# One decoder layer on one core: the keys' weights split during the values' products, first weight sums in another ring, a store and an activation moved, one head filled evenly

## The chip, the cores and the metric

The kernel runs on one core of a Trainium2 chip. The metric is device time in microseconds (us) of one execution, the median of several. TensorE (PE) multiplies matrices, ScalarE (ACT) and VectorE (DVE) work elementwise, GpSimd (POOL) does a few small jobs, and SyncE (SP) issues nearly all DMA transfers. Each engine runs its own instructions in the order in which the program lists them and waits on semaphores for the others.

## The reference

One decoder layer over 1024 tokens of width 1024, all in float32. Cut to what matters here:

```python
h = rms_norm(x, norm_mix_pre)
proj = h @ w_in          # 1024 x 7168: queries, keys, values, pool, memory queries, gate logits
q_d, k_d, v_d, u_p, q_m, gate_logits = split(proj)
# 8 heads; two softmax maps per head, distances as a bias, causal
s = einsum(q, k) * 64 ** -0.5 - slope[head] * (qpos - kpos);  s = where(qpos >= kpos, s, -big)
a = softmax(s)[map 0] - lam * softmax(s)[map 1];  a = rms_norm(a @ v_d) * (1 - lam_init)
gates = sigmoid(gate_logits)                       # 3 branches x 1024
mix = gates[0] * (a @ w_attn_branch) + gates[1] * pool_branch + gates[2] * memory_branch
x = x + rms_norm(mix @ w_out)
x = x + rms_norm((gelu(g) * v) @ w_down)           # [g | v] = conv3(rms_norm(x) @ w_up)
```

The change concerns the projections of values, queries and keys and the start of the attention. Nothing that is computed changes.

## The kernel before

**Float32 by halves.** A float32 operand is split by `split` into a high part, written by ACT as a copy in the matmul's format (L86, or L89 with a scale), and a low part, written by DVE as the rest (L87, L90). `mm3` (L94 to L96) then makes one product out of three matmuls: high by high, high by low, low by high. A *page* is the pair of high and low parts of one piece of weights. Pages live in the pool `wst`, in two rings named "wh" and "wl", two buffers each, used in turn by the counter `pages`; `wst` also has the ring "raw" (two buffers) for weights as loaded.

**Seven products.** Large projections use the seven-product scheme of Strassen and Winograd (`seven`, products named B11, T1, T2, B22, T3, B21, T4 in its order): `weight_sums` (L193 to L196, DVE) makes four sums of weight blocks, `product` splits a page and runs its twelve matmuls, and L211 to L223 bring the results from the accumulators into a tile.

**The stages around the change**, in order of time:
- *Gate pairs* (loop up to L622): sigmoid gates of the pool and memory branches, stored as `mixp_d` (L622).
- *Values* (L632 to L708, about 419 to 496 us). The value weights `vw` (four tiles of 1 MB) are loaded at L632. `value_product` runs seven products (B11, B21, T2, T1, T3, B22, T4), each with four pages (`vpage`) of twelve matmuls. Between them DVE makes sums of weights (`value_combination`, L657) and of results (L682 and others), and `value_out` splits results (`vhl`, `vout`) and stores them to `v_d` (L673).
- *Channels* (L710 to L744, about 496 to 623 us). `channels` loads two weight blocks (`rawq`, L715), makes their sums and runs `seven`: one pair for the keys of two heads, four pairs for the queries, one pair C_G for the first gate logits of the attention branch. The four sums lie in two tiles of ring "t" of pool `gq`, the ring that `value_out` uses for most of its `vhl` tiles too. `split_heads` splits a pair's result and stores it to `k_d` or `q_d` (L726). After each of the last three query pairs `key_weights` is called twice (heads 2 to 7): load a 512 KB block (`rawk`, L731), split it (`whl`, ring "g" of `gp_`), store 1 MB to `wk_d` (L734). These weights are read back during the attention, where the keys of heads 2 to 7 are computed. C_G's result `gq` is stored by POOL (L744).
- *Attention* (from about 623 us), head by head. POOL writes the table of distances `bias` (iota L756, then a mask L758); ACT scales it to `hbias` for each head (L763). `scores` runs the score matmuls into `pss` (L869, two maps), DVE adds `hbias` and finds the extreme (L872), ACT takes the exponential (L877). `combine` (L888 to L891) joins the maps, `turn_weights` transposes (L907), `weigh_values` multiplies by the values (L924), `head_norm` sums squares (L942). `weave` runs a head's stages and puts *fillers* between them: other work that keeps PE occupied. Head 0 has 22 stages and four fillers, two that load values and two that run the gate projection `gate(2)` (matmuls into `pg`); the parameter `over` = 10 has them all placed by the tenth stage. For the first scores SP loads `q`, `ks` (L798), then raw gate weights (L325), `v` and the next queries, in this order.

**What sets the order.** The code is written in loops; a scheduler places each instruction on its engine's list, and pools decide by their rings which tile waits for which. A tile of a ring can be written when all readers of the tile that had its buffer before are done, stores included. Completed transfers are counted on semaphores; SP's and ACT's transfers use eight of them in turn, DMAHW0 to DMAHW7, and the next transfer on one of them is issued only when the last one on it has landed. POOL's transfers have others.

## Time and profile before

| | |
|---|---|
| median of 3 runs | 1771.48 us (1771.41 to 1773.68) |
| the profiled execution | 1771.9 us, span 1770.0 us |
| PE busy | 1723.3 us, 97% of the span |
| DVE, ACT, POOL busy | 72%, 50%, 3% |
| mean granted TensorE clock | 0.993 of full speed |

The span runs from the first to the last instruction of the profiled execution; 1.9 us of its time lie around it. PE is busy nearly all the time, so a time is saved where PE waits or where its clock is low, and lost where either is new. The profile gives for each engine what it did, how long it sat idle ahead of a group of instructions and what it waited for (the *releaser*), and for each stretch the clock that was granted to PE.

### The profile page before, as it was taken

The page shows a single profiled execution, that of the slowest core. Times are in us where ns is not written, and L with a number is a line of the kernel's source. Part 1 is how long each engine was busy: PE and PEld are TensorE (multiplying, and loading weights), DVE is VectorE, ACT ScalarE, POOL GpSimd, SP SyncE. Part 2 cuts the span into 40 slices and gives each one's busy share as a digit, 9 for nine tenths or more (in the row PEclk, how much of TensorE's full clock was granted, in tenths as well). Part 3 has the DMA queues.
Part 4 walks back from the last instruction along what each step waited for, and adds up shares of the span by engine and source line. Part 5 has one row for each costly group of instructions (what it writes and reads, how often), then busy time and mean ns, then how long its engine had stood idle before and what let it go on. Part 6 is the DMA issues. An engine that isn't in the chain of part 4 may idle for free.

```text
span 1770.0 us, 22594 instructions
## 1 busy us (share of the span) xinstructions
PE 1723.3 (97%) x8138; PEld 1427.6 (81%) x8138; DVE 1274.0 (72%) x2221; ACT 885.7 (50%) x1544; POOL 45.9 (3%) x104
## 2 busy tenths in 40 slices
PE   6999999999989989999999999999999999999997
PEld 5888888888868768888887888888888888888886
DVE  7875875666556657888865557857888888878476
ACT  6434454434434457777743333555555555643452
POOL 0000000000000011111110000000000000000000
PEclk9999999999999989999999999999999999999999
DMA  7783544453357975765556482274333323483343
GB/s 243 250 321 129 181 149 131 163 162 120 109 161 254 288 207 165 195 162 156 158 169 226 156 251 72 102 227 153 93 122 119 110 88 107 172 305 101 112 141 138
DMA packets 230517, 294.94 MB, mean 167 GB/s; under 512 B 15761, under 2 KB 161414, under 8 KB 226950
## 3 DMA queue, kind: packets, MB, share of 16 engines
q1 hardware_dynamic: 226614, 285.08, 50.9%
q0 software_dynamic: 3792, 8.43, 1.3%
q8 instruction: 64, 1.05, 0.2%
q14 instruction: 47, 0.39, 0.1%
HBM read 201.62 MB, written 85.56 MB: 162 GB/s over the span
## 4 chain that ended last, share of the span: by engine, by line
PE 73%; issue 13%; DVE 4%; DMA 4%; ACT 2%; POOL 2%; SPq 0%; POOLq 0%; DVEq 0%; ACTq 0%
PE pa L94 8%; PE pa L96 8%; PE pa L95 8%; PE pb L94 5%; PE pb L96 5%; PE pb L95 5%; PE pya L96 2%; PE pe L96 2%; PE pe L95 2%; PE pe L94 2%; PE pya L94 2%; PE pya L95 2%; PE pd L94 2%; PE pd L95 2%; PE pd L96 2%
## 5 line engine op out<-in xcount | busy, mean ns | idle before, releaser
L86 ACT ACTIVATE wpage<-s 128x512 fp32r<-128x512 f32 x144 | 90.3, 628 | 105.9 <-DVE s L193 42.9
L87 DVE TENSOR_TENSOR wpage<-s,wpage 128x512 fp32r<-128x512 f32 x144 | 97.8, 689 | 45.1 <-ACT wpage L86 45.1
L1241 DVE SCALAR_TENSOR_TENSOR cvt<-gv,cols,cvt 128x1023 f32<-128x1023 f32 x88 | 112.5, 1278 | 15.7 <-ACT cvt L1237 15.7
L872 DVE CUSTOM_DVE_ANT_0 z<-pss,hbias 128x256 f32<-128x256 f32 (+7 forms) x128 | 94.8, 753 | 35.8 <-PE pss L869 27.1
L877 ACT ACTIVATE z<-z,mx 128x256 f32<-128x256 f32 (+7 forms) x128 | 99.1, 775 | 17.4 <-DVE mx L872 16.4
L94 PE MATMUL pa<-T,wpage 128*128 128x512 f32 x264 | 102.8, 389 | 0.8 <-DVE gv L244 0.8
L96 PE MATMUL pa<-T,wpage 128*128 128x512 f32 x264 | 102.7, 389 | 0.0
L95 PE MATMUL pa<-T,wpage 128*128 128x512 f32 x264 | 102.7, 389 | 0.0
L869 PE MATMUL pss<-ks,q 128*128 128x512 f32 (+5 forms) x384 | 89.7, 357 | 7.3 <-DVE mx L872 7.1
L86 ACT ACTIVATE page<-blk 128x1024 fp32r<-128x1024 f32 (+1 forms) x42 | 41.5, 990 | 85.9 <-PE pe L95 50.6
L869 PEld LDWEIGHTS pss<-ks,q 128*128 128x128 f32 x384 | 63.6, 193 | 18.4 <-DVE mx L872 14.0
L87 DVE TENSOR_TENSOR page<-blk,page 128x1024 fp32r<-128x1024 f32 (+1 forms) x42 | 47.7, 1136 | 39.3 <-ACT page L86 39.3
L86 ACT ACTIVATE wh<-raw 128x1024 fp32r<-128x1024 f32 (+1 forms) x46 | 41.9, 911 | 65.5 <-issue 16.6
L94 PE MATMUL pd<-page 128*128 128x512 f32 x176 | 68.6, 390 | 1.4 <-ACT row L1351 1.4
L96 PE MATMUL pd<-page 128*128 128x512 f32 x176 | 68.5, 389 | 0.0
L95 PE MATMUL pd<-page 128*128 128x512 f32 x176 | 68.5, 389 | 0.0
L94 PE MATMUL pa<-hT,wpage 128*128 128x512 f32 x168 | 65.7, 391 | 0.4 <-ACT gq L211 0.2
L96 PE MATMUL pa<-hT,wpage 128*128 128x512 f32 x168 | 65.4, 389 | 0.0
L95 PE MATMUL pa<-hT,wpage 128*128 128x512 f32 x168 | 65.4, 389 | 0.0
L924 PEld LDWEIGHTS poa<-aT,v 128*128 128x128 f32 x480 | 61.4, 192 | 4.2 <-ACT srow L944 2.0
L924 PE MATMUL poa<-aT,v 128*128 128x256 f32 (+1 forms) x480 | 63.6, 282 | 0.0
L87 DVE TENSOR_TENSOR wl<-raw,wh 128x1024 fp32r<-128x1024 f32 (+1 forms) x46 | 47.6, 1036 | 17.6 <-ACT wh L86 17.5
(409 smaller groups left out, 5048.3 us busy)
## 6 DMA issues: line engine op xcount, KB each, us to landing
q<-q_d SPq DMA_DIRECT2D x64, 256.0 KB, 4.8
wd<-in_w_down_dram SPq DMA_DIRECT2D x22, 512.0 KB, 5.3
tw_d<-wd SPq DMA_DIRECT2D x11, 1024.0 KB, 4.6
rawv<-in_w_up_dram SPq DMA_DIRECT2D x22, 512.0 KB, 5.6
rawu<-in_w_up_dram SPq DMA_DIRECT2D x22, 512.0 KB, 4.1
ff_d<-cvt SPq DMA_DIRECT2D x22, 512.0 KB, 4.4
blk<-ff_d SPq DMA_DIRECT2D x20, 512.0 KB, 7.1
br<-tw_d SPq DMA_DIRECT2D x20, 512.0 KB, 3.7
```

The lines of the kernel that those rows point to most:

```text
L86: nc.scalar.activation(out=hi, in_=src, func=AF.Copy)
L87: nc.vector.tensor_tensor(out=lo, in0=src, in1=hi.bitcast(F32), op=ALU.subtract)
L94: nc.tensor.matmul(o, ah, bh, start=first, stop=False, skip_group_check=onto)
L95: nc.tensor.matmul(o, ah, bl, start=False, stop=False, skip_group_check=onto)
L96: nc.tensor.matmul(o, al, bh, start=False, stop=last, skip_group_check=onto)
L869: nc.tensor.matmul(pss[:, i * H:i * H + m], q[:, j, c, ts], keys, start=(j == 0), stop=(j == 1))
L872: nc.vector.tensor_tensor_reduce(out=halves(z[:, 0:n]), in0=pss.rearrange("p (a m) -> p a m", a=2)[:, 0:parts, 0:m], in1=halves(biases[h][ ...
L877: nc.scalar.activation(out=z[:, 0:n], in_=z[:, 0:n], func=AF.Exp, scale=-1.0, bias=mx[:, c:c + 1], accum_out=sm if c else sums[:, h, t:t + 1])
L924: nc.tensor.matmul(po[:, qs], (vh, vl)[i][:, k, :], w[j][:, ws], start=(n == 0), stop=(n == len(terms) - 1))
L1241: nc.vector.scalar_tensor_tensor(out=cv[:, sh:], in0=u[:, 0:S - sh], scalar=w, in1=cv[:, sh:], op0=ALU.mult, op1=ALU.add)
```

## The change

1. `key_weights(h)` is called during the values instead of the channels: after B11 for head 2, then after B21, T2, T1, T3 and B22 for heads 3 to 7. The block is split in two halves into pages (`kpage`) of the rings "wh" and "wl", the rings of the value pages, and each half is stored on its own (512 KB, L666).
2. The four weight sums of the first pair (keys) lie in a tile `ss` of ring "y" of `gp_` instead of two tiles of ring "t".
3. The store of C_G's result to `gate_d` is issued from ACT's queue (L756 in the new numbering) instead of POOL's.
4. An activation `warm` (an exponential of one column) is written after the gate pairs.
5. `weave` loses `over`: head 0's four fillers are spread over its 22 stages.

```diff
-    def weave(stages, fillers, over=None):
+    def weave(stages, fillers):
-            want = min((i + 1) * len(fillers) // (over or len(stages)), len(fillers))
+            want = (i + 1) * len(fillers) // len(stages)
...
+        warm = small.tile([P, 1], F32, tag="sm", name="warm")
+        nc.scalar.activation(out=warm, in_=nlam, func=AF.Exp)
...
+        def key_weights(h):
+            raw = wst.tile([P, KT, P], F32, tag="raw", name="rawk", bufs=2)
+            nc.sync.dma_start(out=raw, in_=chunk(w_in, C_K + h * P))
+            for e in range(2):
+                page = wst.tile([P, 2, H4, P], F32R, tag=("wh", "wl")[pages[0] % 2], name="kpage")
+                pages[0] += 1
+                ks = slice(e * H4, (e + 1) * H4)
+                split(page[:, 0], page[:, 1], raw[:, ks])
+                nc.sync.dma_start(out=wk_d[h, :, :, ks], in_=page.bitcast(F32))
...
         value_product("B11", vblock(*A11), va, True)
+        key_weights(2)
...
         value_product("B21", vblock(*A12), vb, True)
+        key_weights(3)
...
         value_product("T2", vblock(*A11), va, False)
+        key_weights(4)
...
         value_product("T1", vblock(*A21), vb, True)
+        key_weights(5)
...
         value_product("T3", vblock(*A11), va, False)
+        key_weights(6)
...
         value_product("B22", vblock(*A12), vb, False)
+        key_weights(7)
...
-        def channels(c0, tag="g"):
+        def channels(c0, tag="g", ss=None):
...
-            s12, s43 = [gq.tile([P, 2, H4, P], F32, tag="t", name="s") for _ in range(2)]
-            seven(raws, (s12[:, 0], s12[:, 1], s43[:, 0], s43[:, 1]), hop, g)
+            if ss is None:
+                s12, s43 = [gq.tile([P, 2, H4, P], F32, tag="t", name="s") for _ in range(2)]
+                ss = (s12[:, 0], s12[:, 1], s43[:, 0], s43[:, 1])
+            seven(raws, ss, hop, g)
...
-        def key_weights(h):
-            raw = wst.tile([P, KT, P], F32, tag="raw", name="rawk", bufs=2)
-            nc.sync.dma_start(out=raw, in_=chunk(w_in, C_K + h * P))
-            whl = gp_.tile([P, 2, KT, P], F32R, tag="g", name="whl", bufs=3)
-            split(whl[:, 0], whl[:, 1], raw)
-            nc.sync.dma_start(out=wk_d[h], in_=whl.bitcast(F32))
-
-        split_heads(channels(C_K), k_d)
+        ss = gp_.tile([P, 4, H4, P], F32, tag="y", name="ss")
+        split_heads(channels(C_K, ss=[ss[:, j] for j in range(4)]), k_d)
         for h in range(0, NH, 2):
             split_heads(channels(h * P), q_d[h:h + 2], -0.125)
-            if h:
-                for e in range(2):
-                    key_weights(h + e)
...
-        nc.gpsimd.dma_start(out=gate_d[0:2].rearrange("e p s -> p e s"), in_=g)
+        nc.scalar.dma_start(out=gate_d[0:2].rearrange("e p s -> p e s"), in_=g)
...
-        weave(stages, fillers, 10 if h == 0 else None)
+        weave(stages, fillers)
```

The built programs show where this puts instructions. First, DVE at the step from the values' second product (B21) to the third (T2). Before, where `vw_3558` and `vw_3559` are T2's weights, `vpage_3705` to `vpage_3750` its four pages, and L682 adds B21's results:

```order
L87 TENSOR_TENSOR vpage_3682<-vw_3561,vpage_3682 128x512
L657 TENSOR_TENSOR vw_3559<-vw_3559 128x2x512
L87 TENSOR_TENSOR vpage_3705<-vw_3558,vpage_3705 128x512
L87 TENSOR_TENSOR vpage_3720<-vw_3558,vpage_3720 128x512
L682 TENSOR_TENSOR vtmp_3562<-ve_3569,vtmp_3562 128x512
L682 TENSOR_TENSOR vtmp_3562<-ve_3571,vtmp_3562 128x512
L682 TENSOR_TENSOR vtmp_3562<-ve_3570,vtmp_3562 128x512
L682 TENSOR_TENSOR vtmp_3562<-ve_3572,vtmp_3562 128x512
L87 TENSOR_TENSOR vpage_3735<-vw_3559,vpage_3735 128x512
```

Now T2's first pages are `vpage_3727` and `vpage_3742`, L698 is the same addition, and `kpage_3711` and `kpage_3715` are the halves of head 3's key weights:

```order
L87 TENSOR_TENSOR vpage_3694<-vw_3563,vpage_3694 128x512
L87 TENSOR_TENSOR kpage_3711<-rawk_3709,kpage_3711 128x512
L671 TENSOR_TENSOR vw_3561<-vw_3561 128x2x512
L87 TENSOR_TENSOR kpage_3715<-rawk_3709,kpage_3715 128x512
L698 TENSOR_TENSOR vtmp_3564<-ve_3571,vtmp_3564 128x512
L698 TENSOR_TENSOR vtmp_3564<-ve_3573,vtmp_3564 128x512
L698 TENSOR_TENSOR vtmp_3564<-ve_3572,vtmp_3564 128x512
L698 TENSOR_TENSOR vtmp_3564<-ve_3574,vtmp_3564 128x512
L87 TENSOR_TENSOR vpage_3727<-vw_3560,vpage_3727 128x512
L87 TENSOR_TENSOR vpage_3742<-vw_3560,vpage_3742 128x512
```

T2's first two low parts stood ahead of the four additions and stand behind them now.

Second, SP's list at the first scores, with what each transfer waits for. Before, `ks_4963` and `ks_4964` are head 0's keys for the two maps:

```order
L798 DMA ks_4963<-k_d 64x1024 [waits DMAHW2_49]
L798 DMA ks_4963<-k_d 64x1024 [waits DMAHW3_49]
L798 DMA ks_4964<-k_d 64x1024 [waits DMAHW4_49,DVE_49]
L798 DMA ks_4964<-k_d 64x1024 [waits DMAHW5_49]
L325 DMA raw<-in_w_in_dram 128x8x128 [waits DMAHW6_49]
L776 DMA v<-v_d 128x1024 [waits DMAHW7_49,PE_49]
```

Now they are `ks_4988` and `ks_4989`:

```order
L810 DMA ks_4988<-k_d 64x1024 [waits DMAHW1_49]
L810 DMA ks_4988<-k_d 64x1024 [waits DMAHW2_49]
L810 DMA ks_4989<-k_d 64x1024 [waits DMAHW3_49,DVE_49]
L810 DMA ks_4989<-k_d 64x1024 [waits DMAHW4_49]
L325 DMA raw<-in_w_in_dram 128x8x128 [waits DMAHW5_49]
L788 DMA v<-v_d 128x1024 [waits DMAHW6_49,PE_49]
```

And ACT's list at the same place, now (before, it is the same without the DMA, with the last L223, two `hbias`, the table load and the first exponential in a row):

```order
L215 ACTIVATE gq_4838<-pa_4845 128x512 [waits PE_49]
L86 ACTIVATE wpage_4944<-rawq_4836 128x512 [waits DMAHW1_49]
L223 ACTIVATE gq_4838<-pa_4845 128x512 [waits DVE_49,PE_49,Activation_49]
L756 DMA gate_d_91<-gq_4838 128x2x1024 [waits DVE_49,Activation_49]
L775 ACTIVATE hbias_4994<-bias_4973 128x1152 [waits Pool_49]
L775 ACTIVATE hbias_5042<-bias_4973 128x1152
L889 ACT_TABLE_LOAD
```

The store took a place among the transfers that count on DMAHW0 to DMAHW7: it counts on DMAHW4, and the second half of `ks_4989` now waits until that count shows the store landed. On POOL's list the DMA ahead of the iota is gone. The table load ahead of the first exponential is still there; `warm` has gone to ACT's 44th instruction, far ahead of the sigmoids' table load.

Third, PE in the middle of head 0. Before, `pg_5111` is the second half of the gate projection, `pss_5131` to `pss_5192` are scores:

```order
L95 MATMUL pg_5111<-hTl_111,wh 128x512
L96 MATMUL pg_5111<-hTh_109,wl 128x512
L869 MATMUL pss_5131<-ks_4963,q 128x320 x4
L869 MATMUL pss_5139<-ks_4964,q 128x320 x4
L94 MATMUL pg_5111<-hTh_109,wh 128x512
L95 MATMUL pg_5111<-hTl_111,wh 128x512
L96 MATMUL pg_5111<-hTh_109,wl 128x512
```

Nine more of these gate matmuls follow before the next transposes. Now the second half is `pg_5275`, and the scores are `pss_5142` to `pss_5230`:

```order
L881 MATMUL pss_5189<-ks_4989,q 128x384 x4
L95 MATMUL pg_5275<-hTl_111,wh 128x512
L96 MATMUL pg_5275<-hTh_109,wl 128x512
L94 MATMUL pg_5275<-hTh_109,wh 128x512
L881 MATMUL pss_5230<-ks_4988,q 128x448 x3
```

What stood in a block is now three matmuls at a time, up to the end of the head. The list of PE is the same in both programs again from early in head 1.

## Rows read from the trace of the kernel before

**Rows 1.** PE's waits, 420 to 670 us: total in us, times, longest

```profile
PE pss L869 <- DVE mx L872: 6.5, 3, 5.4
PE pb L94 <- ACT wpage L86: 6.4, 1, 6.4
PE pta L907 <- DVE aT L87: 1.2, 3, 0.7
PE pa L96 <- DVE wpage L87: 1.1, 1, 1.1
PE pa L94 <- ACT wpage L86: 1.1, 1, 1.1
PE pta L907 <- DVE z L891: 0.5, 1, 0.5
```

**Rows 2.** Stretches: us; PE, PEld, DVE, ACT, POOL busy; clock, DMA share, GB/s

```profile
460.00:480.00 20.00, 20.00 (x90) 16.57 (x89) 8.96 (x14) 8.65 (x15) 0.00 (x0) 1.00 0.20 54
...
500.00:505.00 5.00, 0.00 (x0) 0.00 (x0) 2.54 (x4) 1.23 (x2) 0.00 (x0) 0.80 0.85 236
505.00:510.00 5.00, 4.98 (x12) 3.89 (x13) 3.71 (x7) 1.86 (x3) 0.00 (x0) 0.52 0.01 3
...
560.00:610.00 50.00, 47.55 (x207) 38.13 (x206) 34.70 (x47) 27.43 (x40) 0.00 (x0) 1.00 0.97 323
...
628.40:636.40 8.00, 7.25 (x19) 5.41 (x20) 5.72 (x22) 6.84 (x17) 0.00 (x0) 0.52 1.03 351
...
660.00:664.00 4.00, 4.00 (x18) 3.62 (x19) 3.83 (x12) 3.86 (x10) 0.51 (x1) 0.57 0.99 227
```

**Rows 3.** Timeline, first pair: start, duration, instruction, [idle before <-releaser]

```profile
503.61 0.69 DVE L193 TENSOR_TENSOR s<-rawq 128x512 f32<-128x512 f32 x1 [1.29 <-DMA v_d<-vhl]
```

**Rows 4.** Key weights' splits: duration min/median/max in ns, first and last start

```profile
L86 ACT ACTIVATE whl<-rawk x6: 1054/1062/1073, 546.7 to 593.3; 128x1024 fp32r<-128x1024 f32 x6
L87 DVE TENSOR_TENSOR whl<-rawk,whl x6: 1215/1224/1227, 547.8 to 594.4; 128x1024 fp32r<-128x1024 f32 x6
```

**Rows 5.** Timeline of DVE at the end of the product B21

```profile
439.69 2.73 DVE L682 TENSOR_TENSOR vtmp<-ve,vtmp 128x512 f32<-128x512 f32 x4 [0.41 <-PE ve L96]
442.34 1.28 DVE L87 TENSOR_TENSOR vpage<-vw,vpage 128x512 fp32r<-128x512 f32 x2
```

**Rows 6.** Line 673's view: SP's 256 KB stores of values to v_d

```profile
DMA to landing us min/median/max: 2.3/2.6/3.7
```

**Rows 7.** Line 726's view: SP's 1 MB stores to k_d and q_d

```profile
DMA to landing us min/median/max: 3.9/5.3/6.2
```

**Rows 8.** Timeline of ACT late in the channels

```profile
603.81 0.63 ACT L86 ACTIVATE wpage<-rawq 128x512 fp32r<-128x512 f32 x1 [1.32 <-DMA rawq<-in_w_in_dram]
```

**Rows 9.** Timelines of ACT, POOL, DVE and PE at the attention's start

```profile
622.71 0.60 ACT L223 ACTIVATE gq<-pa 128x512 f32<-128x512 f32 x1 [8.90 <-PE pa L96]
626.89 2.22 ACT L763 ACTIVATE hbias<-bias 128x1152 f32<-128x1152 f32 x2 [3.58 <-POOL bias L758]
629.13 1.28 ACT L877 ACT_TABLE_LOAD   x1
...
623.62 0.88 POOL L744 DMA_DIRECT2D gate_d<-gq  x1 [572.63 <-ACT gq L223]
...
628.09 0.29 DVE L872 CUSTOM_DVE_ANT_0 z<-pss,hbias 128x128 f32<-128x128 f32 x1 [7.45 <-ACT hbias L763]
...
633.04 0.63 PE L94 MATMUL pg<-hTh,wh 128*128 128x512 f32 x1
```

**Rows 10.** Line 798's view: SP's loads of ks from k_d, 256 KB

```profile
DMA to landing us min/median/max: 4.3/10.7/11.6
```

**Rows 11.** DMA view, 420 to 670 us: the load of raw gate weights

```profile
raw<-in_w_in_dram SPq DMA_DIRECT2D x1, 512.0 KB, 5.9
```

**Rows 12.** Tile view of ks, all its loads of the run

```profile
DMA to landing us min/median/max: 2.2/4.0/11.6
```

**Rows 13.** Timeline of DVE in head 0

```profile
641.40 0.69 DVE L872 CUSTOM_DVE_ANT_0 z<-pss,hbias 128x512 f32<-128x512 f32 x1 [4.75 <-PE pss L869]
```

## The prediction

> **What bounds the kernel now.** I read the busy shares first: PE works in 97% of the span, so nothing that another engine saves counts unless PE waits for it. The second view is the list of PE's waits between 420 and 670 us, the stretch whose order the change touches [rows 1]; the list of PE is the same again after it. It holds three places. One wait of 6.4 us stands in the first pair of channels: the page of its first weight sum comes late. One of 5.4 us (of 6.5 in three) stands at the first scores, for DVE's extremes. Waits of 1.1 and 1.1 us stand late in the channels, and some 2.2 us of short ones (1.2, 0.5, and the remaining 0.5 beside the 5.4 and one of 0.6) lie at the end of head 0. The third view is the table of stretches [rows 2]: it shows what each wait costs beyond itself. Between 460 and 480 us, 90 matmuls take 20.00 us at full clock, 0.222 us each. After the first wait the granted clock is 0.52, near 1.2 GHz where 1.00 is 2.4 GHz, and 12 matmuls take 4.98 us. After the wait at the first scores it is 0.52 too, and in 660 to 664 us 0.57. All sums are made against the profiled execution, 1771.9 us; the median is 0.4 us lower, and I take that off at the end. 0.2%, or 3.5 us, is about what a measurement of this kernel can tell from no change.
>
> **The first pair's sums.** DVE's first sum starts at 503.61, released by the landing of a store of `vhl` [rows 3]: the sums lie in the ring that the last value stores still hold. In the new ring they wait for nothing of the last product; their raw weights are loaded later than before, but need to land only some 3 us ahead of the end of T4, and the order shows the sums ahead of T4's end. The wait goes whole: 6.4 us, and with it the clock's cost, 4.98 - 12 x 0.222 = 2.3 us [rows 1, 2]. **-8.7 us**. What is late next there is nothing on PE's path before the second product, whose page is split from sums that are ready. If the new ring's earlier readers should hold the sums, the value products before them hide up to 10 us of that.
>
> **The key weights' splits, moved.** Each costs ACT 1.06 and DVE 1.22 us [rows 4], six times; halved, they are twelve of about 0.64 and 0.69 (the value pages' own size). In the values DVE is busy 8.96 us of 20 and ACT 8.65 [rows 2], so the sum of 13.7 us of engine time (6 x 2.28) over 70 us hides behind PE, which stays dense. It costs only where a split stands in the order ahead of something PE is about to need:
> - *B21 to T2.* DVE's first addition of B21's results is released by PE's first finished accumulator at 439.69, and the four end at 442.42 [rows 5]; nine matmuls, 2.0 us, remain to PE at the first release, so PE reaches T2 near 441.4. Before, T2's first low parts were made by then. Now they stand behind the additions: the first is there at 442.42 + 0.64 = 443.06, and PE, with two high-by-high matmuls to spend (0.45 us), waits from 441.85, which is 1.2 us; the half key page ahead of the additions can add 0.7. I take 1.5; the ends are 0.5 (the scheduler's slack) and 2.9 (both key halves in the way).
> - *B11 to B21.* The second half of the value weights is loaded behind one more load, and the splits of head 2's halves stand ahead of the sum that follows: I take 0.5, ends 0 and 1.5. The other four steps have slack of a page; together 0.3.
>
> Together **+2.3 us**, ends 0.8 and 5.
>
> **Their stores, moved.** Six loads of 0.5 MB and twelve stores of 0.5 MB leave a stretch with a DMA share of 0.97 for one with 0.20 [rows 2]. SP gives each some 0.35 us, which nobody waits for as SP is not full there. But the pages lie in the rings of the value pages, so seven later pages each wait until a 512 KB store has landed. By the order such a page is wanted some 5.3 us after the store's issue (two pages of twelve matmuls, 12 x 0.222 = 2.7 us each). The trace does not show a 512 KB store there; the bounds are the 256 KB stores of the same stage, 2.3 to 3.7 us [rows 6], and the 1 MB stores of the next, 3.9 to 6.2 [rows 7]. I take 3.5, nearer to the former since the traffic is that of the former: no wait. At 6.2, five products would lose 0.9 each, 4.5 us; this is the high end.
>
> **Late in the channels.** ACT waits at 603.81 for a load of `rawq` [rows 8], which came late behind the key weights' loads and stores in the same ring and the same crowded stretch. With these gone the next pair's weights are loaded a pair ahead. 1.1 + 1.1 go [rows 1]; new is that C_G's first result waits until a `q_d` store has landed, 3.9 to 6.2 us against about 5.4 that it has: 0 to 0.8, taken as 0.2. **-2.0 us**.
>
> **The store on ACT, distances early.** Before, POOL's list was held until L223 was done, then by its own DMA: 0.88 us from 623.62, then iota and mask, and `hbias` ran at 626.89, and DVE began at 628.09 [rows 9]. Now iota and mask stand free, `hbias` follows L223 near 623.8, about 3 us earlier. That alone is worth 3.0 us. But the store now takes DMAHW4, and SP's second load of the second map's keys waits for it to land. Let T be the end of C_G's matmuls, near 622.6. L223 ends at T + 0.7; the store is issued by T + 1.0 and lands 3.9 to 6.2 later (5.0 taken) [rows 7]; the load is issued by T + 6.5 and lands 2.2 later at the least [rows 12], 4.3 at the least among the first loads [rows 10], 3.0 taken since the queue behind it is empty when it starts. So PE has the second map's keys at T + 9.5 (ends T + 7.6 and T + 12). From DVE's start to the gate matmuls it took 4.95 us before (628.09 to 633.04 [rows 9]), of which the first two extremes would now be done: 4.2 remain, so the gate matmuls start near T + 13.7. The raw gate weights, issued behind that load, agree: T + 7 + 5.9 [rows 11] + 1.0 for their split, T + 13.9. Before it was T + 10.4. In place of a gain of 3.0 the place loses **+3.1 us**, ends -3.0 (no wait) and +5.8. Queued behind the waiting load on SP are the raw gate weights, the values and the next queries; PE waits for the first two. The low clock after the wait is paid in either kernel.
>
> By the Trainium skill (DMA: Bandwidth & Descriptors, Anatomy of one DMA), a transfer on the POOL path takes about 2.0 us plus its bytes over 436 GB/s, an estimate of 4.4 us for 1 MB. Rows 7 have 5.3 as the median for stores issued by SP; with 4.4 in place of 5.0 this place would cost 2.5 and the time would be 0.6 lower.
>
> **Even filling.** Before, DVE sits idle 4.75 us for scores while PE runs gate matmuls in a block [rows 13], and at the end of the head PE waits for DVE, 2.2 us in all [rows 1], with the clock at 0.57 in four microseconds, at most 4.00 x 0.43 = 1.7 us of loss [rows 2]. Now the second half of the gate projection is spread, so DVE has its scores earlier and PE has matmuls left for the end. The first block still stands where it was, so the 4.75 us stay mostly; DVE remains 3.83 of 4.00 us busy there. Ends 0 and -3.9; I take **-2.7 us**.
>
> **The activation `warm`.** The table load of 1.28 us ahead of the first exponential [rows 9] is still in ACT's list, and `warm` stands hundreds of instructions ahead of the sigmoids, so it changes nothing: 0. The wait for `ks` would hide the load now anyway.
>
> **Sum.** -8.7 + 2.3 - 2.0 + 3.1 - 2.7 = -8.0. 1771.9 - 8.0 - 0.4 = 1763.5 us.
>
> **Rivals.**
> - *The store's wait is hidden.* If SP's load finds the store landed when PE wants the keys, the early `hbias` counts whole: -3.0 in place of +3.1, and the time is 1757.4. For it: SP's earlier loads might run late enough by themselves [rows 10]. Against: the order has the load directly behind loads that need only C_G's last low part. The Trainium skill (DMA: Bandwidth & Descriptors, Issuing engines are not separate DMA queues) says that issuing from several engines only saves the sequencer's issue time; by this the store's move alone would be worth the 0.88 us of POOL and no more, 1759.5. No row shows a DMA issued by ACT. Chance 0.2.
> - *The gains are eaten.* The even filling brings nothing, because DVE is as full in either order, and the steps between the value products cost 5 us: -8.7 + 5 - 2.0 + 3.1 = -2.6, 1768.9, and with the late ends at the first scores up to 1771.5. For it: DVE's 3.83 of 4.00 [rows 2]. Chance 0.17.
> - *The key pages hold the value products* (the other side). If a 512 KB store takes longer than 5.3 us to land while it shares the stage with loads and the stores of values, each of five products waits for the rest, and each wait can lower the clock. At 9 us this is 5 x 3.7 = 18.5 us: 1782. It decides from where 5 x (landing - 5.3) exceeds the 8.0 us: 6.9 us. Against: no SP store above takes over 6.2 us, even in the crowded stretch. Chance 0.07.
>
> **How the numbers follow.** The forecast has 0.56, with 1760 to 1767 as its own range; the first rival 0.20, the second 0.17, the third 0.07. Faster by over 0.2% (below 1768): the forecast, the first rival, and a little of the second: 0.78. Within 0.2%: most of the second, 0.15. Slower: the third, 0.07. The range from 1756.5 to 1771 takes in the first rival and nearly all of the second, and leaves out the third and the far ends.
>
> **What would show it.** Right: no wait of PE before the second product of the first pair, the clock at 1.00 there; `hbias` near 624; the second pair of score matmuls waiting for `ks` and not for DVE; the table load still ahead of the first exponential; no wait of a value page for a store. Wrong: value pages released by `wk_d` stores; a new wait at the first pair; PE waiting for DVE at the end of head 0 as long as before.

## The result, and the profile after

The changed kernel takes 1760.98 us (median of 4 runs, 1760.41 to 1761.98) against 1771.45 us of before on the same chip: a ratio of 0.9940, with an interval of 0.9923 to 0.9957. That is 10.5 us less; 1763.5 was forecast, with 1756.5 to 1771.0 as the range. The profiled execution took 1760.41 us with a span of 1758.4 us, 11.6 us under the span of before.

PE's waits from 415 to 665 us in the changed kernel (total, times, longest) answer to [rows 1]:

```profile
PE pss L881 <- DMA ks<-k_d: 8.7, 1, 8.7
PE vd L95 <- DVE vpage L87: 0.9, 1, 0.9
PE pss L881 <- DVE mx L884: 0.8, 2, 0.5
PE pa L94 <- ACT gq L211: 0.7, 1, 0.7
PE pta L919 <- DVE z L903: 0.7, 1, 0.7
PE pta L919 <- ACT sq L942: 0.2, 1, 0.2
```

The 6.4 us at the first pair are gone, as are the two of 1.1 late in the channels, and the short ones at head 0's end are fewer (the last four rows but the one for `gq`, 1.7 us, where 2.4 were). One wait is larger than before: the first scores now wait 8.7 us, and for a load of `ks`, not for DVE. The stretches (us; PE, PEld, DVE, ACT, POOL busy; clock, DMA share, GB/s) answer to [rows 2]:

```profile
440.00:460.00 20.00, 19.07 (x85) 15.44 (x84) 15.71 (x23) 10.56 (x20) 0.00 (x0) 1.00 0.86 268
460.00:480.00 20.00, 20.00 (x90) 16.57 (x89) 10.69 (x17) 10.98 (x19) 0.00 (x0) 1.00 0.56 175
...
500.00:505.00 5.00, 5.00 (x23) 4.13 (x22) 1.64 (x3) 2.60 (x5) 0.00 (x0) 1.00 0.78 219
505.00:510.00 5.00, 5.00 (x24) 4.13 (x23) 2.99 (x5) 2.47 (x5) 0.00 (x0) 1.00 0.95 258
...
618.00:622.00 4.00, 0.00 (x0) 0.00 (x0) 0.00 (x0) 0.54 (x3) 0.00 (x0) 0.56 0.69 150
622.00:626.00 4.00, 3.78 (x11) 2.83 (x12) 2.23 (x12) 2.58 (x8) 0.00 (x0) 0.50 1.01 326
```

PE runs through the first pair at full clock; 500 to 510 us hold 47 matmuls where before they held 12. The values' stretch moves more (a DMA share of 0.86 and 0.56 where 460 to 480 had 0.20), and PE stays dense there but for one wait. Only the first scores have a low clock, 0.50 when PE goes on.

To see where the time went I take the starts of PE's matmuls in both timelines as marks, since the order of PE's list hardly differs. Each line is the time from its mark to the next:

| from | before | after | difference | forecast |
|---|---|---|---|---|
| start to the values' first product | 418.9 | 419.1 | +0.2 | 0 |
| values, to the first product of the first pair | 76.9 | 78.7 | +1.8 | +2.3 |
| first pair, to its product B21 | 22.6 | 13.6 | -9.0 | -8.7 |
| to the product B21 of C_G | 98.7 | 96.4 | -2.3 | -2.0 |
| C_G's B21 to the first gate matmul | 16.0 | 18.9 | +2.8 | +3.1 |
| heads, to the branch projection | 311.6 | 308.0 | -3.5 | -2.7 |
| branch projection | 90.2 | 87.7 | -2.5 | 0 |
| the rest | 735.2 | 736.1 | +0.9 | 0 |

The five places that the prediction names are each within 0.9 us of their terms and sum to -10.2 where -8.0 was forecast. The branch projection, which the change does not touch, gave another 2.5; a second trace of before, below, settles whose they are.

The place that got worse, the first scores, as the timelines have it (start, us, instruction, idle before and releaser):

```profile
613.21 0.33 PE L881 MATMUL pss<-ks,q 128*128 128x128 f32 x2
622.22 4.60 PE L881 MATMUL pss<-ks,q 128*128 128x128 f32 x12 [8.67 <-DMA ks<-k_d]
626.62 0.63 PE L94 MATMUL pg<-hTh,wh 128*128 128x512 f32 x1
...
613.46 0.60 ACT L223 ACTIVATE gq<-pa 128x512 f32<-128x512 f32 x1 [9.81 <-PE pa L96]
614.09 0.39 ACTq L756 DMA_DIRECT2D gate_d<-gq  x1
614.53 2.22 ACT L775 ACTIVATE hbias<-bias 128x1152 f32<-128x1152 f32 x2 [0.47 <-ACT gq L223]
616.76 1.28 ACT L889 ACT_TABLE_LOAD   x1
618.05 0.40 ACT L889 ACTIVATE z<-z,mx 128x128 f32<-128x128 f32 x1
...
604.40 14.14 SPq L810 DMA_DIRECT2D ks<-k_d  x2
618.59 0.59 SPq L325 DMA_DIRECT2D raw<-in_w_in_dram  x1
```

`hbias` starts 1.1 us after L223 does, where [rows 9] has 4.2. But SP stands between its last two key loads until about 618, some 4 us after the store was issued on ACT at 614.09, the raw gate weights leave only at 618.59, and the keys let PE go on at 622.22.

### The profile page after: what moved, and what is told of

Same layout as the page of the kernel before. It is cut to its first block, busy times and chain, and to the rows that moved or that the text cites. A ratio compares the mean times of both kernels' runs of the same rounds, so it can differ in the third digit from the quotient of the medians.

```text
span 1758.4 us, 22637 instructions
## 1 busy us (share of the span) xinstructions
PE 1716.7 (98%) x8138; PEld 1424.0 (81%) x8138; DVE 1273.5 (72%) x2227; ACT 884.1 (50%) x1551; POOL 45.4 (3%) x103
## 4 chain that ended last, share of the span: by engine, by line
PE 82%; DVE 8%; DMA 4%; issue 3%; ACT 2%; SPq 0%; POOL 0%; DVEq 0%; ACTq 0%; POOLq 0%
PE pa L94 8%; PE pa L96 8%; PE pa L95 8%; PE pb L94 5%; PE pb L96 5%; PE pb L95 5%; PE pss L881 2%; PE pe L95 2%; PE pe L94 2%; PE pe L96 2%; PE pya L94 2%; PE pya L96 2%; PE poa L936 2%; PE pya L95 2%; PE pd L94 2%
## 5 line engine op out<-in xcount | busy, mean ns | idle before, releaser
L86 ACT ACTIVATE wpage<-s 128x512 fp32r<-128x512 f32 x140 | 87.7, 627 | 111.6 <-DVE s L193 37.4
L881 PE MATMUL pss<-ks,q 128*128 128x512 f32 (+5 forms) x384 | 90.7, 357 | 10.5 <-DMA ks<-k_d 8.7
L87 DVE TENSOR_TENSOR wl<-raw,wh 128x1024 fp32r<-128x1024 f32 (+1 forms) x46 | 47.6, 1035 | 19.0 <-ACT wh L86 18.9
```

What stands on the lines that cost most here:

```text
L86: nc.scalar.activation(out=hi, in_=src, func=AF.Copy)
L87: nc.vector.tensor_tensor(out=lo, in0=src, in1=hi.bitcast(F32), op=ALU.subtract)
L881: nc.tensor.matmul(pss[:, i * H:i * H + m], q[:, j, c, ts], keys, start=(j == 0), stop=(j == 1))
```

## The experiments

### The store on POOL again, in the changed kernel

```diff
-        nc.scalar.dma_start(out=gate_d[0:2].rearrange("e p s -> p e s"), in_=g)
+        nc.gpsimd.dma_start(out=gate_d[0:2].rearrange("e p s -> p e s"), in_=g)
```

> The changed kernel with C_G's store issued by POOL again; all else as changed. My theory: in the changed kernel the second load of the second map's keys waits on SP because it shares a completion count with the store on ACT, and PE's 8.7 us at the first scores are that. With the store on POOL the count is another, the wait for ks goes, POOL's iota stands behind the store again, and the place costs what it did before the change: a wait of about 5.4 us for the extremes, and the gate matmuls start 10.4 us after C_G's end in place of 13.2. Time about 2.8 us under the changed kernel's 1761.0, 1758.2 us. Rival (the keys are late because SP's queue is crowded, whoever issues the store): the wait for ks stays at 8 us or more and the time is 1761 or above.

1760.05 us (ratio to before 0.9941, 0.9929 to 0.9953). The wait for `ks` is gone, and the old one is back:

```profile
PE pss L881 <- DVE mx L884: 6.8, 4, 5.4
PE pa L94 <- ACT wpage L86: 1.0, 1, 1.0
```

From C_G's B21 to the first gate matmul it takes 16.0 us, 2.8 less than the changed kernel. So the wait was the store's place. In the whole time 0.9 us of it show, and the ratios cannot be told apart: 1.0 went to a page that came late in the channels here (the second row), and 0.5 to the heads. The clock accounts for the 0.5: over the 10 us from the first gate matmul its mean is 0.85 here and 0.90 in the changed kernel.

### The store on ACT, head 0's first queries loaded by POOL

```diff
-    queries(0, 0)
+    queries(0, 0, nc.gpsimd)      # the engine that issues the four loads
```

> The changed kernel with head 0's first four query loads issued by POOL in place of SP; the store stays on ACT. Nothing is taken from SP's crowd but four short loads, yet the counts turn by four, and the key loads share theirs with stores of queries that landed long ago. My theory (the shared count): PE's wait for ks goes, hbias stays early, the scores go on about 2.5 us after C_G's end, and the gate matmuls start 7 to 8 us after it in place of 13.2: about 1755.5 us. Rival (the keys are late because of the crowd on SP or in the DMA engines): at most 1 to 2 us less than the changed kernel, about 1760 us. A second rival is that POOL's loads land late: then PE waits for q, and the time is 1758 to 1763.

1759.56 us (0.9940, 0.9926 to 0.9953). The key loads are no longer held: they are all issued by 604.7, nearly nine us ahead of the store, and land in 4.3 to 6.8 us. The rows are PE's waits and the two landings:

```profile
614.46 0.41 PE L881 MATMUL pss<-ks,q 128*128 128x128 f32 x2 [1.89 <-issue]
618.91 1.20 PE L881 MATMUL pss<-ks,q 128*128 128x128 f32 x4 [4.04 <-issue]
...
DMA to landing us min/median/max: 4.3/6.4/6.8
...
DMA to landing us min/median/max: 3.8/5.4/12.2
```

The shared count is the cause, then: nothing was taken from SP's crowd but four short loads, and SP was no longer held between two key loads. But the second rival came true with it: POOL issued the queries at 604.5 to 607.1, into the raw weights and the values that SP was loading, and the last of them (the second landing row is that of all queries) took up to 12.2 us, so PE waited 1.9 and 4.0 us: two of these loads land at 614.4 and 618.7, where the waits end. The first gate matmul comes 5.9 us earlier than in the changed kernel, and the heads give back 3.5 of that. The clock accounts for 1.3 of the 3.5: its mean over the 10 us from the first gate matmul is 0.77, where the changed kernel has 0.90. The other 2.2 are not explained by any run.

### Only the store moved, in the kernel before

> The kernel before with only its store of C_G's result moved from POOL to ACT. In this program too the last of the four key loads shares its count with that store. My theory: slower by about 2.8 us than before, 1774.3 us, with PE waiting some 8 us for ks. Rival (the early distances outweigh it): 3.0 us faster, 1768.5 us.

1771.35 us against 1770.19 (1.0007, 0.9995 to 1.0019): no change that can be told, where 2.8 us were expected. PE's first wait at the scores is for `ks` here too:

```profile
PE pss L869 <- DMA ks<-k_d: 8.4, 1, 8.4
```

The first gate matmul comes 2.6 us later than in the trace of before, as expected, and the heads then take 2.3 us less than in that trace, and 1.4 less than in the second trace of before, below. The clock accounts for that. It is low behind the wait at the scores in each of these traces. Where the gate matmuls start later, more of that low clock has passed while PE waited. Here are the 10 us from the first gate matmul, before and then in this run:

```profile
633.04:643.04 10.00, 10.00 (x42) 7.85 (x42) 4.71 (x14) 4.04 (x12) 0.56 (x1) 0.85 0.45 155
...
635.01:645.01 10.00, 10.00 (x49) 8.00 (x48) 5.47 (x17) 4.20 (x11) 1.01 (x2) 1.00 1.06 234
```

Before loses 1.5 us to the clock in them (10.00 x 0.15; the second trace of before has 0.80, so 2.0), and this run nothing. In the first trace of before the clock also fell at the end of head 0 [rows 2], 1.7 us more; here it did not. By both traces the clock is worth more than what the heads gave back.

### The distances made early, loaded by SP; head 3's key weights later

```diff
+            bias0 = xa.tile([P, 1152], F32, name="bias0", bufs=1)     # in the memory stage
+            nc.gpsimd.iota(bias0, ...); nc.gpsimd.affine_select(out=bias0, ...)
+            nc.gpsimd.dma_start(out=bias_d, in_=bias0)
...
-        nc.scalar.dma_start(out=gate_d[0:2].rearrange("e p s -> p e s"), in_=g)
+        nc.gpsimd.dma_start(out=gate_d[0:2].rearrange("e p s -> p e s"), in_=g)
...
-    nc.gpsimd.iota(bias, ...); nc.gpsimd.affine_select(out=bias, ...)
+    nc.sync.dma_start(out=bias, in_=bias_d)
...
-        key_weights(3)                     # ahead of the additions of B21's results
+                if mid and k == 1:         # in value_product, for T2: after its second page
+                    key_weights(mid)
```

> The changed kernel with three edits: the table of distances is made by POOL during the memory stage, kept in device memory and loaded by SP; C_G's store is issued by POOL; head 3's key weights are split in the middle of T2 instead of ahead of it. My theory: no transfer at the first scores shares a count with the store, and nothing of the distances waits for it, so DVE has hbias 2.4 us after C_G's end and the keys of both maps, the gate matmuls start 6 to 7 us after C_G's end in place of 13.4, and the step from B21 to T2 is free again, 1.3 us: about 1755.5 us. Rival (head 0 is bound by DVE's and ACT's own chain of scores, so an earlier start is given back by its end): 1758.5 us.

1755.50 us (0.9912, 0.9898 to 0.9925), 5.5 us under the changed kernel and what the theory said to the tenth; the exactness is luck. At the first scores (PE, ACT, SP):

```profile
614.98 4.50 PE L886 MATMUL pss<-ks,q 128*128 128x128 f32 x12 [2.02 <-DMA ks<-k_d]
...
613.06 2.21 ACT L780 ACTIVATE hbias<-bias 128x1152 f32<-128x1152 f32 x2
...
601.63 0.32 SPq L776 DMA_DIRECT2D bias<-bias_d  x1
```

PE waits 2.0 us there in place of 8.7, and the first gate matmul comes 7.0 us after C_G's end where the changed kernel has 13.4. The heads take 308.6 us, nearly the changed kernel's 308.0, so the gain is kept this time. The values take 0.7 us less. Of the two theories it was the first. Three edits were made at once, so the whole time does not price them one by one; the marks do, as far as their places are apart.

### The same with `warm` behind the sigmoids

```diff
-        nc.scalar.activation(out=warm, in_=nlam, func=AF.Exp)
+        nc.scalar.activation(out=warm, in_=mix[:, 0, 0:1], func=AF.Exp)
```

> The kernel with the distances' table loaded (e7_table_loaded), in which the activation warm reads the last gate pair's result and so stands behind the sigmoids: the table of the exponential is loaded in the values, and no table load stands ahead of the first exponential. My theory: there, nothing hides the 1.28 us of the load any more, the first exponential and the gate matmuls behind ACT's split come 1.3 us earlier, and 0.5 to 1.3 us remain at the end of head 0: 1754.5 us against 1755.5. Rival (the wait of the second map's keys hides it there too): 1755.5.

1753.75 us (0.9912, 0.9898 to 0.9925): the ratio is that of the last, so the times do not tell the two apart. The trace shows what the load costs:

```profile
613.69 2.21 ACT L780 ACTIVATE hbias<-bias 128x1152 f32<-128x1152 f32 x2
615.80 0.39 ACT L894 ACTIVATE z<-z,mx 128x128 f32<-128x128 f32 x1
```

The first exponential follows `hbias` directly, 2.85 us after C_G's end where the last kernel has 4.26 (616.58 against 612.32). The first gate matmul does not come earlier (7.2 us after C_G's end against 7.0), since PE waits 2.1 us for the keys in this one too; from C_G's end to the branch projection it is 1.0 us less.

### The changed kernel without `warm`

> The changed kernel without the activation warm. My theory: no change, 1761.0 us, with the table load in the same place. Rival (the early load of the table spares something somewhere): about 1.3 us slower.

1761.59 us (0.9950, 0.9936 to 0.9963), no change that can be told, and the table load stands where it stood:

```profile
614.85 2.21 ACT L773 ACTIVATE hbias<-bias 128x1152 f32<-128x1152 f32 x2 [0.47 <-ACT gq L223]
617.09 1.28 ACT L887 ACT_TABLE_LOAD   x1
618.38 0.40 ACT L887 ACTIVATE z<-z,mx 128x128 f32<-128x128 f32 x1
```

### Only the sums' ring, in the kernel before

> The kernel before with the first pair's weight sums in the other ring and nothing else. My theory: the wait of 6.4 us and the low clock behind it are the ring alone, so all of the 8.9 us that the first pair gained in the changed kernel's trace comes: about 1761.5 us against 1770.2 of before on the last chip. Rival (the key weights' move is needed too, since the sums' raw weights share a ring with them): a wait of 3 us or more stays, 1765 us or above. A second rival is that the earlier end of the channels is given back at the first scores or at head 0's end: 1764 us.

1763.63 us against 1771.51 (0.9964, 0.9951 to 0.9978): 7.9 us by the medians, 6.4 by the ratio (3.9 to 8.7), so more than half of the whole change by either, from the place of one tile. It is less than the 8.9 us of the theory and near the second rival's 1764, though not by its way. The first pair takes 13.6 us to its B21, as in the changed kernel, so the ring alone took the wait and its clock away. 2.5 us are given back late in the channels, where the short waits of before are still there and the clock fell behind them in this execution, at a loss of 1.7 us (4.00 x 0.10 + 4.00 x 0.32):

```profile
596.00:600.00 4.00, 2.61 (x9) 1.82 (x10) 3.87 (x7) 2.50 (x5) 0.00 (x0) 0.90 1.02 376
600.00:604.00 4.00, 4.00 (x14) 3.20 (x13) 0.69 (x1) 1.12 (x2) 0.00 (x0) 0.68 1.02 247
```

### Only the key weights moved, in the kernel before

> The kernel before with the key weights' splits moved into the values and stored by halves, and nothing else. My theory: the values take 1.9 us more (the step from B21 to T2 and the later second half of the value weights), the late channels 2.4 us less, and the first pair's wait stays: 0.5 us faster than before, 1769.7 us. Rival (the first pair's wait comes from the crowd of transfers that the key weights' move thins out): 1763 us. Rival on the other side (value pages wait for the stores): slower than before by over 2 us.

1771.89 us against 1771.51 (1.0009, 1.0000 to 1.0018): by itself the move is worth nothing, or costs up to 3 us, where a gain of 0.5 was expected. Late in the channels it gains 2.5 us; the values take 2.3 more; and the first pair's wait grows. As before, its first sum waits for a store of `vhl`, which lands later now: the sum starts 9.4 us after the pair's first matmul (507.40 against 498.01), where it was 7.9:

```profile
PE pb L94 <- ACT wpage L86: 7.9, 1, 7.9
...
507.40 0.69 DVE L193 TENSOR_TENSOR s<-rawq 128x512 f32<-128x512 f32 x1 [1.97 <-DMA v_d<-vhl]
```

### Each half page stored twice

```diff
                 nc.sync.dma_start(out=wk_d[h, :, :, ks], in_=page.bitcast(F32))
+                nc.sync.dma_start(out=wk2_d[h, :, :, ks], in_=page.bitcast(F32))
```

> The changed kernel in which each half page of key weights is stored twice, the second time to memory that nobody reads, so that a page comes free only when both have landed. It prices the late landing. By the prediction's step (a page is wanted 5.3 us after its store is issued), landings of 9 to 10 us would cost five products 4 us each: some 1780 us. My theory now, from the changed kernel's landings of 6.3 us median and 9.1 at most without a wait of PE: ACT makes pages some 3 us ahead of PE's need, so PE waits only for what passes 9 us: 1761 to 1766 us.

1776.37 us against 1771.51 (1.0026, 1.0016 to 1.0036): 15 us over the changed kernel and slower than before, far above the 1761 to 1766 that I had come to expect and near the 1780 of the prediction's step, but not by its way. PE's waits in values and first pair:

```profile
PE pb L94 <- ACT wpage L86: 7.8, 1, 7.8
PE vd L95 <- DVE vpage L87: 2.0, 1, 2.0
PE vd L94 <- ACT vpage L86: 1.7, 1, 1.7
```

The values cost 5.0 us (83.7 against 78.7), most of it 2.8 more of waits, and 1.7 of a low clock behind the first of them (4.00 x 0.43, from 445 to 449 us). Three pages were held until a store had landed, a key page (8.9 us after its store was issued) and two value pages (4.9 and 5.7 us after the second store of each), and PE waited for none of these three directly; what made its two waits longer stays open. Landings of 9 us at a value page did not come about, so this run does not price them. The larger part, 10.0 us, is the first pair, whose wait is back though its sums lie in the new ring:

```profile
502.56 3.55 SPq L689 DMA_DIRECT2D v_d<-vhl  x4
506.16 0.87 SPq L737 DMA_DIRECT2D rawq<-in_w_in_dram  x1
...
511.72 0.69 DVE L193 TENSOR_TENSOR ss<-rawq 128x512 f32<-128x512 f32 x1 [1.02 <-DMA rawq<-in_w_in_dram]
```

The pair's second load of `rawq` leaves at 506.16, behind value stores on SP's list, and the first sum waits for it until 511.72. In the changed kernel the same load left at 487.31, and the first sum stood at 492.64. The other side is real, then, but it decides at SP's queue more than at the pages' ring.

### Only the even filling, in the kernel before; and the change without it

> The kernel before with head 0's fillers spread evenly and nothing else. My theory: the end of head 0 gains by itself, since the 2.2 us of waits for DVE and the low clock after them go: 3.5 us faster, 1768.0 us, ends 2.7 and 3.9. Rival (the gain at head 0 seen in the changed kernel comes from the later start of the scores, by which the transfers of head 0 and 1 have landed): within 1 us of 1771.5.

1769.54 us against 1770.19 (0.9990, 0.9980 to 1.0000), less than the theory, and at the edge of what can be told: between nothing and 3.5 us. The heads take 309.6 us to the branch projection, 2.0 less than in the first trace of before and 1.1 less than in the second, below. The theory that the low clock at the end of head 0 goes with the even filling is wrong: here it fell there all the same, as in the first trace of before and not as in the second.

```profile
662.00:666.00 4.00, 3.88 (x15) 3.23 (x16) 3.48 (x11) 2.18 (x7) 0.00 (x0) 0.57 0.62 250
```

That is 1.7 us (4.00 x 0.43). With it left out on both sides, the heads are 2.0 us shorter than in the first trace and 2.8 shorter than in the second.

> The changed kernel with head 0's four fillers placed by the tenth stage again; all else as changed. It prices the even filling inside the change. By the prediction it is worth 2.7 us: 1763.7 against 1761.0 of the changed kernel. By the traces of the kernels without it so far (65.4 to 66.0 us from the first gate matmul to the 48th key matmul of head 2 where the clock fell once, 67.1 in the trace of before where it fell a second time at the end of head 0, 63 with even filling) it is worth 1 to 2 us: 1762 to 1763. Rival (nothing, since the head's end waits for DVE in either): 1761.

1763.89 us (0.9963, 0.9951 to 0.9976) against 1760.98: 2.9 us by the medians, where the prediction had 2.7. The two ratios to before make it 4.1, and the run without `warm`, measured on the same chip, 2.3 (1763.89 - 1761.59). The heads take 310.6 us, 2.6 more than with even filling. So inside the change the filling is worth about what was forecast. In the kernel before, the whole time allows 0 to 3.5 us, so no other worth is shown there.

### The kernel before, a second time

> The kernel before once more, for a second trace. In the first one 384 matmuls of the branch projection came 0.2334 us apart after a wait of 0.5 us, where the traces of the changed kernel and of all the experiments have 0.2289, and the clock fell a second time at the end of head 0. If both belong to the kernel, they are there again; if they belong to that execution, the branch projection shows 0.2289, or head 0's end full clock, and the profiled execution is up to 3 us shorter.

1771.58 us, span 1769.7: 0.3 us under the first profiled execution, not 3. Yet both oddities of the first trace were that execution's: the branch projection runs at the usual spacing, and the clock did not fall at head 0's end. It fell late in the channels instead, behind the short waits there, and cost 3.4 us (8.00 x 0.43, the first row):

```profile
605.00:613.00 8.00, 6.86 (x18) 5.09 (x17) 3.93 (x7) 3.08 (x6) 0.00 (x0) 0.57 1.04 291
660.00:664.00 4.00, 2.76 (x17) 2.03 (x17) 3.93 (x7) 2.85 (x6) 0.00 (x0) 1.00 0.65 158
985.00:1000.00 15.00, 15.00 (x67) 12.33 (x66) 6.67 (x9) 4.44 (x7) 0.00 (x0) 1.00 0.51 155
```

With this trace as before, the stretches differ from the changed kernel's by 1.7 (values), -9.5 (first pair), -5.4 (late channels, with the low clock), +2.8 (first scores), -2.7 (heads) and -0.1 us (branch projection).

## Why the prediction was right, point by point

**The first pair.** -8.7 forecast, -9.0 and -9.5 measured against the two traces of before. The cause was the ring alone, as put (only the ring: the wait gone). What the prediction did not see is its condition: the raw weights must leave SP's queue in time, and with the stores doubled they did not.

**The splits in the values.** +2.3 forecast, +1.8 measured. The wait stands where it was put, at T2's first low part, 0.9 us where 1.5 was taken. The prediction's own row gives 0.9 without the half key page: nine matmuls, 2.0 us, from 439.69 are 441.7, and the text went on with 441.4. With head 3's key weights split in the middle of T2 this wait is gone, and the values take 0.7 us less than in the changed kernel, still 1.1 more than before.

**The stores' landing.** 3.5 us was taken for a store of 512 KB, and it held where a value page waited for one. Below are the view of all twelve stores, ACT's rows with the waits, and SP's rows with the stores (each row the two halves of one head, the second some 2.7 us behind the first):

```profile
DMA to landing us min/median/max: 3.6/6.3/9.1
...
461.67 0.63 ACT L86 ACTIVATE vpage<-vw 128x512 fp32r<-128x512 f32 x1 [1.16 <-DMA wk_d<-kpage]
472.82 1.29 ACT L86 ACTIVATE vpage<-vw 128x512 fp32r<-128x512 f32 x2 [1.43 <-DMA wk_d<-kpage]
...
458.54 3.24 SPq L666 DMA_DIRECT2D wk_d<-kpage  x2
469.42 3.23 SPq L666 DMA_DIRECT2D wk_d<-kpage  x2
```

ACT's four waits for these stores, 4.7 us in all, end 3.1 to 3.7 us after the stores were issued (461.67 - 458.54 and 472.82 - 469.42 for the first halves). PE takes up these two pages only at 465.11 and 475.99, and so never waited. The view's first line must not be read as a median of twelve: the trace has the landing of two of them, 9.1 and 3.6 us. The expectation for the doubled stores was built on that median. The two halves of head 2 took 9.1 and 9.2, since the move fills that stretch (a DMA share of 0.96 from 430 to 440 us, where before it was 0.39); they held two key pages for 1.1 us together, and no value page. So one sign of being wrong did show, value pages released by `wk_d` stores, but at ACT and not at PE. The other step, that a page is wanted 5.3 us after its store, was short: PE takes those pages up 6.6 us after the issue (465.11 - 458.54), and ACT needs 0.6 of that. The rival on the other side, 18.5 us for landings of 9 us, is not priced by any run; what it left out is SP's queue, where the doubled stores cost the first pair 10.0 us.

**Late in the channels.** -2.0 forecast, -2.3 measured against the first trace of before, with the new wait for `q_d` at 0.7 in place of 0.2. Against the second trace it is -5.4. What was not in the sum is that the clock sometimes falls behind the short waits there, at a loss of 3.4 us in that execution; in the traces with the key weights moved it stays at 1.00 there.

**The first scores.** +3.1 forecast, +2.8 measured. `hbias` came early, and the shared count took more than it gave, by the steps named: PE got the second map's keys 9.0 us after C_G's end (613.2), where 9.5 was put, and the gate matmuls came 13.4 us after it, where 13.7 was put. That 9.0 came so near 9.5 is in part luck: the last key load left 4.9 us after C_G's end, where 6.5 was put, and took 4.1 us, where 3.0 was put. A slip of 0.2 is in the sum too, since 13.7 less the 10.4 of before is 3.3 and not 3.1. The runs with the store on POOL and with the queries on POOL show the cause by two ways.

What the prediction missed is that a later start of the gate matmuls costs less by the end of the heads than at its place, since the low clock behind the wait then passes in part while PE waits. With only the store moved the heads gave back 2.3 or 1.4 of 2.6 us, and the clock accounts for that; with POOL's store it accounts for the 0.5 of 2.8; with POOL's query loads it accounts for 1.3 of the 3.5 given back of 5.9. With the keys of both maps and `hbias` there early, 5.9 of 6.4 us were kept to the branch projection. Whether the rest of head 0 also goes at the pace of DVE's and ACT's chain of scores is not shown by any run.

The rule of the Trainium skill (DMA: Bandwidth & Descriptors, Issuing engines are not separate DMA queues), that an issue from another engine saves only the sequencer's time, fits the whole times: with the store on ACT or POOL they cannot be told apart. It does not tell of the wait that a shared completion count brings, which is 8.7 us in the trace; from C_G's B21 to the branch projection the store on POOL is 2.4 us shorter.

**Even filling.** -2.7 forecast, 2.3 to 4.1 measured by taking it away, -3.5 in the stretch of the traces and -2.7 against the second trace of before. The first trace's low clock at the end of head 0, which the prediction counted in, is not shown to go with the filling: it fell with even filling too, and did not fall in the five other traces without it.

**`warm`.** 0 forecast, 0 measured; where it does what it says, 1.4 us earlier for the first exponential.

The Trainium skill (ScalarE: Activation LUTs, What ACT_TABLE_LOAD costs) has 1.28 us for the load and 1.38 more for a drain. The trace agrees with the first (616.76 to 618.05) and shows no drain: `hbias` ends at 616.75 and the exponential starts at 618.05.

**The sum.** The named places give -10.2 by the first trace of before, where no term is off by over a microsecond; 10.5 is the difference of the medians, 2.5 more than the forecast. By the second trace they give -13.1, with the late channels 3.4 us off, as much as the low clock cost there. So the terms were right in their mechanism, and the sum left out that the kernel before loses some microseconds more to short waits, now in one place and now in another. That the 2.5 us are this is likely from the traces, not shown. The 2.5 us of the branch projection in the table belong to one execution of before: in the second trace the stage takes as long as in the changed kernel.

## What to carry to other kernels

Ask of every transfer that moves to another queue which completion count it takes, and which later transfers must now wait for it: here a store that nobody read for 300 us held the keys that the next stage began with. A wait for a store's landing can be a matter of the ring alone: one tile in another ring was more than half of this change. Moving transfers into a quiet stage makes parts of it busy, so look for the stretch that fills, and at what stands behind them on the issuing queue. Ask of a median how many landings it rests on. And before a stretch that became shorter is called a gain, or one that became longer a loss, look at the clock on either side of its marks.

## What the runs showed of the hardware that was not expected

A group of short waits can bring the clock to 0.50 behind it, or not, in executions of the same kernel. In the first trace of before it fell at the end of head 0, behind 1.2 us of waits, in the second late in the channels, and with the store alone moved at neither. Late in the channels, waits of 1.0 and 1.1 us brought it down in the run with only the sums' ring, and the same two did not in the run with only the store moved. Such waits can cost 1.7 or 3.4 us more than their own length, or nothing more.

In the first trace of before the 384 matmuls of the branch projection came 0.2334 us apart, at full clock, behind a wait of 0.5 us; in the second, and in the trace of the changed kernel and of every experiment, 0.2289 us. This stretch of the first trace has 66 matmuls, where the same stretch of the second, above, has 67:

```profile
985.00:1000.00 15.00, 15.00 (x66) 12.16 (x65) 7.21 (x10) 4.53 (x7) 0.00 (x0) 1.00 0.42 140
```

It is 1.7 us over the stage (383 x 0.0045). The wait is not the cause: with only the store moved PE waits 0.5 us for the same page there, and the spacing is 0.2289. Why one execution kept the slower spacing is not settled by any run here.
